# Serving the second layer's experts with 64 tokens each and no branches, the rest through the loop

## The chip, the cores and the metric

The kernel runs on one core of one Trainium2 chip. The metric is the device time of one execution in microseconds; three runs of the kernel before gave 1768.14, 1769.0 and 1769.58 us, median 1769.0.

## What is computed

Two layers of a transformer over 512 tokens and 256 context tokens of width 1024 in float32. Each layer has a mixer (attention beside a convolution or a pooling), then a mixture of experts. The part that matters here is the experts:

```python
def _moe(h, grp_w, grp_b, exp_w, exp_b, w_gate, w_up, w_down):
    ...
    hid = jax.nn.silu(xb @ w_gate[e]) * (xb @ w_up[e])
    return (hid @ w_down[e]) * wt[:, None]
```

There are 32 experts in 4 groups; a token takes one group and two experts of it, whose results are weighted and added. In the last layer only the 512 tokens take part: 1024 assignments, 32 an expert on average. Every expert's weights are read whole: gate and up 1024x512 each, down 512x1024, 6 MB in float32, 32 times in each layer.

## The kernel before

The weights of an expert are loaded as 12 tiles of 128x1024 float32, 512 KB each: chunks 0 and 1 (4 tiles each) hold gate and up, chunk 2 (4 tiles) holds down. They go to places of 4 KB a partition (`Pages`); a place that is given back by `used` is taken by the next load in the order of use (`ahead`, L1326 on), issued by SP (L1333) or, at the start, in part by ACT. The pool of the experts adds `NS[l]` places to those that are lasting; in layer 1 there are 3.

All engines but SP keep, in this stage, the order in which the program is written (`by_hand`); nothing reorders the instructions of an engine. `main` (the loop over `n` in `range(NE)`) takes the experts one after another, two experts (a pair, index `m`) sharing one gather:

- `gather0(m)` (POOL, L1352): the rows of up to 64 tokens of each of the pair's experts, one below the other in `Xg`. `gather1` does so for tokens 65 to 128, under a branch.
- `trans(m, b)` (`transposed`, L1460): 8 transpositions on PE into PSUM `xtp`, and 8 evictions by ACT (L689) and DVE (L687) in turn, with the norm's gain and shift, into `xt`. Block `b = 1` is transposed whether it holds tokens or not.
- `mm_gate_up(0, ...)` (L1476): per weight tile two products of 64 columns (32 records of a 128x512 float32 product an expert, as each product has two passes), then a branch on the expert's count for the second block.
- `hidden` (ACT L1481, DVE L1482) and `hidden_T` (4 transpositions L1489, copy L1494): the activation of both blocks, turned for the next product.
- `down(n - 1)` (L1500): the previous expert's down products, one expert behind. In layer 1 then `result` (DVE L1386: weight and gate), `parts` (ACT L1408, POOL L1409: the result as a high and a low part that PE multiplies exactly in one pass each), and a branch for a second block (`second`).
- `combine(m)` (L1426): at each even expert, the results of the pair before are added to their tokens: a one-hot matrix (`onehot`, DVE L1413) times high and low part, 8 units of two products, each added to `X` by DVE (L1390).

The last three experts (`TAIL`) have their second blocks deferred to one branch behind the last one. Experts with more than 128 tokens get the rest in the loop of `rest` (L1656 on), entered if the count of such blocks is not zero. `slots` computes each place's weight for both blocks with 16 products `wps` (L1271) before expert 0. A branch on several engines (L1294, L1296) splits the program; what is behind waits for what stands in front on that engine.

Of the kernel before, what the change touches and what calls it, by code (L numbers as in the profile page):

```python
# [7 lines left out]
F32 = mybir.dt.float32  # L8
# [60 lines left out]
def hybrid_dit_kernel(ctx: ExitStack, tc: tile.TileContext, a, out):  # L69
# [56 lines left out]
    def load(src, n=4, pools=None, queue=nc.sync):  # L126
        """The first n pages of a chunk of weights"""
# [75 lines left out]
    def gemv_first(n, w):  # L203
        """The shift and the scale of a pair of row blocks in layer 0's first norm"""
# [19 lines left out]
    def scale_cols(l, which):  # L224
        """ln gain * (1 + scale), one column a block of 128"""
# [8 lines left out]
    def mod_rows(l, name, src):  # L234
        """A vector of columns as rows in DRAM, to be read into all partitions."""
# [9 lines left out]
    def router_bias(l):  # L245
        """The router's logits of the second norm's shift, and its bias"""
# [12 lines left out]
    def rpow(work, ss, n, scale):  # L259
        """1/sqrt(ss * scale + eps)"""  # L260
# [14 lines left out]
    # A float32 is the sum of two parts of 12 bits each, which TensorE multiplies exactly in one pass each;  # L275
    # a product of two float32 takes three passes then: high * high, high * low and low * high.
    class Split:
        """A chunk of weights in its two parts, made page by page by the steps"""
# [20 lines left out]
        def __call__(self, p, k, o, n):  # L299
            """Columns o to o + n of row block k, part p"""  # L300
# [9 lines left out]
    rope = {}  # L310

    def rope_tables(l, pool, t0=0, n=XT):
        """Of tiles t0 to t0 + n"""
# [42 lines left out]
    def qk_rotate(l, t, n0, qn, W, mid):  # L356
        """Rotation and split of the normed queries and keys"""
# [1811 lines left out]
```

## Time and profile before

| what | value |
|---|---|
| runs | 1768.14, 1769.0, 1769.58 us |
| profiled execution, span | 1769.0 us (its own time is the same within the spread of the runs; the span is the median) |
| PE busy | 1567.2 us, 89% |
| PE weight loads (beside the products) | 866.9 us, 49% |
| DVE, ACT, POOL busy | 913.2, 528.4, 427.4 us |
| HBM read | 510.49 MB, 300 GB/s over the span |
| gate/up products, both layers (L1476) | 516.7 us busy, 2304 records |
| down products, both layers (L1500) | 264.8 us busy, 1152 records |

The page cuts the span into 40 slices of 44.2 us. The experts of layer 0 take about 440 to 960 us, those of layer 1 about 1245 to 1769. A busy share is an average over stages; the stage must be looked at by itself, with windows. Waits are listed as "who waited <- whom"; PEq and SPq are the sequencers of PE and SP, which branch and issue DMAs. Idle time shorter than about 0.15 us is not listed as a wait.

### The profile page before, as it was taken

The page shows a single profiled execution, that of the slowest core. Times are in us where ns is not written, and L with a number is a line of the kernel's source. Part 1 is how long each engine was busy: PE and PEld are TensorE (multiplying, and loading weights), DVE is VectorE, ACT ScalarE, POOL GpSimd, SP SyncE. Part 2 cuts the span into 40 slices and gives each one's busy share as a digit, 9 for nine tenths or more (in the row PEclk, how much of TensorE's full clock was granted, in tenths as well). Part 3 has the DMA queues.
Part 4 walks back from the last instruction along what each step waited for, and adds up shares of the span by engine and source line. Part 5 has one row for each costly group of instructions (what it writes and reads, how often), then busy time and mean ns, then how long its engine had stood idle before and what let it go on. Part 6 is the DMA issues. An engine that isn't in the chain of part 4 may idle for free. (4 is left out here: it accounts for less than half of the span.)

```text
span 1769.0 us, 24713 instructions
## 1 busy us (share of the span) xinstructions
PE 1567.2 (89%) x8732; PEld 866.9 (49%) x8732; DVE 913.2 (52%) x1747; ACT 528.4 (30%) x1036; POOL 427.4 (24%) x347
## 2 busy tenths in 40 slices
PE   5979689997899999998986789989799999989997
PEld 4867457885333333332321676677334344343442
DVE  3897889788333232322333656656534445344454
ACT  3422468733111111111112434663312122121221
POOL 1535556132112112211111223201121121111110
PEclk9999799999999999999999899999799999999999
DMA  9121743447999999999998338145699999999992
GB/s 368 58 83 66 292 155 122 164 148 278 354 396 397 388 390 386 391 394 389 392 400 332 123 108 319 58 180 188 257 408 408 408 408 406 408 406 406 405 407 91
DMA packets 151597, 519.03 MB, mean 293 GB/s; under 512 B 22445, under 2 KB 23181, under 8 KB 151437
## 3 DMA queue, kind: packets, MB, share of 16 engines
q1 hardware_dynamic: 134300, 479.67, 69.2%
q0 software_dynamic: 11520, 16.81, 3.7%
q10 hardware_dynamic: 5616, 20.45, 3.0%
q8 instruction: 97, 1.59, 0.4%
q14 instruction: 64, 0.52, 0.1%
HBM read 510.49 MB, written 21.02 MB: 300 GB/s over the span
## 5 line engine op out<-in xcount | busy, mean ns | idle before, releaser
L1476 PE MATMUL gu<-w,xt 128*64 128x512 f32 x2304 | 516.7, 597 | 21.1 <-DMA w<-in_ex_dram 11.9
L1476 PEld LDWEIGHTS gu<-w,xt 128*64 128x64 f32 x2304 | 171.5, 137 | 326.6 <-issue 247.6
L1500 PE MATMUL yy<-w,ht 128*64 128x512 f32 x1152 | 264.8, 601 | 14.2 <-PEq L1296 5.9
L1482 DVE TENSOR_TENSOR hh<-hh,gu 128x512 f32<-128x512 f32 x64 | 44.1, 688 | 451.6 <-ACT hh L1481 451.6
L1481 ACT ACTIVATE hh<-gu 128x512 f32<-128x512 f32 x64 | 38.3, 598 | 566.2 <-PEq L1296 416.2
L1500 PEld LDWEIGHTS yy<-w,ht 128*64 128x64 f32 x1152 | 81.4, 137 | 172.4 <-issue 133.7
L1379 POOL DMA_INDIRECT xD<-ys,sidx x40 | 70.6, 1765 | 317.8 <-DVE ys L1375 315.3
L1409 POOL TENSOR_TENSOR lo<-ys,hi 64x1024 fp32r<-64x1024 f32 x29 | 68.2, 2351 | 325.0 <-ACTq L1296 325.0
L749 DVE SCALAR_TENSOR_TENSOR acc<-glu,convp,acc 128x784 f32<-128x784 f32 x76 | 97.9, 1288 | 1.6
L760 POOL TENSOR_TENSOR part<-part,prod 128x784 f32<-128x784 f32 x40 | 84.7, 2118 | 43.2 <-ACT prod L759 42.2
L1375 DVE TENSOR_TENSOR ys<-yy,ys 128x512 f32<-128x512 f32 x64 | 44.3, 692 | 97.8 <-PEq L1296 53.4
L1408 ACT ACTIVATE hi<-ys 64x1024 fp32r<-64x1024 f32 (+1 forms) x35 | 34.4, 983 | 193.1 <-DVE ys L1386 108.8
L1352 POOL DMA_INDIRECT Xg<-hD,gidx x40 | 42.6, 1066 | 188.9 <-PE xtp L1460 179.7
L264 POOL TENSOR_TENSOR rs<-ms,mhalf 128x1 f32<-128x1 f32 (+2 forms) x40 | 41.5, 1038 | 170.8 <-DVE ms L262 170.3
L1390 DVE TENSOR_TENSOR X<-X,cmb 128x512 f32<-128x512 f32 x126 | 77.0, 683 | 1.6 <-PE cmb L1426 1.1
L1426 PE MATMUL cmb<-hi,oh 128*128 128x512 f32 x128 | 58.0, 453 | 22.2 <-DVE oh L1413 20.5
L1460 PEld LDWEIGHTS xtp<-cst,Xg 128*128 128x128 f32 x512 | 58.0, 146 | 34.6 <-PEq L1296 18.6
L1460 PE MATMUL xtp<-cst,Xg 128*128 128x128 f32 x512 | 64.8, 282 | 9.1 <-PEq L1296 9.1
L522 PE MATMUL ptp<-cst,P 128*128 128x128 f32 x368 | 53.3, 284 | 18.7 <-POOL P L510 10.5
L1494 DVE COPY ht<-htp 128x512 f32<-128x512 f32 x64 | 43.8, 684 | 50.0 <-PE htp L1489 50.0
L695 PE MATMUL qps<-wh,hi 128*128 128x256 f32 (+1 forms) x176 | 61.4, 349 | 8.0 <-DVE hi L1819 2.4
L687 DVE TENSOR_SCALAR xt<-xtp,A,modT 128x128 f32<-128x128 f32 x128 | 49.6, 410 | 35.7 <-ACT xt L689 34.6
(310 smaller groups left out, 2633.9 us busy)
## 6 DMA issues: line engine op xcount, KB each, us to landing
w<-in_ex_dram SPq DMA_DIRECT2D x751, 512.0 KB
w<-in_mod_w_dram SPq DMA_DIRECT2D x96, 512.0 KB
w<-in_ex_dram ACTq DMA_DIRECT2D x17, 512.0 KB
w<-in_w_out_dram SPq DMA_DIRECT2D x16, 512.0 KB
w<-in_w_in_ab_dram SPq DMA_DIRECT2D x14, 512.0 KB
hD<-x ACTq DMA_DIRECT2D x8, 512.0 KB
xD<-X ACTq DMA_DIRECT2D x6, 512.0 KB
w<-in_w_in_cd_dram ACTq DMA_DIRECT2D x6, 512.0 KB
```

The lines of the kernel that those rows point to most:

```text
L522: nc.tensor.transpose(ps[:, (c - c0) * 128:(c - c0 + 1) * 128], u["P"][c // nk][:, c % nk * 128:(c % nk + 1) * 128], ident)
L687: nc.vector.tensor_scalar(dst[:, k, :], src, g, b, op0=OP.mult, op1=OP.add)
L695: nc.tensor.matmul(ps[:, o:o + n], h(x, k, tk), w(p, k, 0, n), start=(k == 0 and c == 0), stop=(k == KT - 1 and c == 2))
L749: nc.vector.scalar_tensor_tensor(acc, glu[:, ct, i:i + CW], w(i), acc, OP.mult, OP.add)
L760: nc.gpsimd.tensor_tensor(self.part[ct], self.part[ct], t, OP.add)
L1379: return nc.gpsimd.indirect_dma_start(out=xD[:, :], out_offset=bass.IndirectOffsetOnAxis(ap=idx, axis=0), in_=ys[:, :], in_offset=None, bo ...
L1390: nc.vector.tensor_tensor(x, x, ps, OP.add)
L1409: eng.tensor_tensor(lo[rows, c], ys[rows, c], hi[rows, c].bitcast(F32), OP.subtract)
L1426: nc.tensor.matmul(ps, oh[:, tok(t)], y[:, c * 512:(c + 1) * 512], start=(i == 0), stop=(i == 1))
L1460: nc.tensor.transpose(ps[:, k * 128:(k + 1) * 128], src[:, (h * 4 + k) * 128:(h * 4 + k + 1) * 128], ident)
L1476: nc.tensor.matmul(self.gu[c * 64:(c + 1) * 64, b, :], xt[:, k, q * 64:(q + 1) * 64], w[k][:, c * 512:(c + 1) * 512], start=(k == 0), stop ...
L1500: nc.tensor.matmul(yy[c * 64:(c + 1) * 64], t[:, b, f % 2, f // 2, :], w[f][:, c * 512:(c + 1) * 512], start=(f == 0), stop=(f == 3))
```

## The change

In layer 1 an expert's own share is one block of 64 tokens (`FIRSTB = (2, 1)`); what is beyond 64 goes to `rest`, which so far served what is beyond 128. With that, layer 1 gets a loop of its own (`main1`) with no branches in it: no second gather, no second transposition, no second gate/up, hidden or down, and one branch behind the last expert. `hidden` and `hidden_T` work on half the columns. Gate/up and down alternate between two halves of their PSUM tiles. The one-hot is made before the down products of the same turn, and the 8 units of `combine` run inside the next expert's gate/up products: two units after each of its tiles 5, 6 and 7, the others behind. The products `wps`, 8 instead of 16, run behind expert 0's gate/up. The pool has 5 places instead of 3. Layer 0 keeps its loop (`main0`) and its order.

```diff
-NS = (9, 3)
+NS = (9, 5)
+FIRSTB = (2, 1)
...
-            pg = sm("pg")[:, :4 * NE]
-            for b in range(2):
+            pg = sm("pg")[:, :2 * self.nb * NE]
+            for b in range(self.nb):
...
-            for c in (slice(0, 512), slice(512, D)) if n >= TAIL else (slice(0, D),):
+            for c in (slice(0, 512), slice(512, D)):
...
-        def mm_gate_up(self, b, xt, q, w):
+        def mm_gate_up(self, b, xt, q, w, beside=lambda k: None):
             for k in range(KT):
                 for c in range(2):
                     nc.tensor.matmul(self.gu[c * 64:(c + 1) * 64, b, :], xt[:, k, q * 64:(q + 1) * 64],
                                      w[k][:, c * 512:(c + 1) * 512], start=(k == 0), stop=(k == KT - 1))
+                beside(k)
-        def hidden(self, nb):
-            hh = self.wp.tile([128, 2, 256], F32, tag="hh", name="hh", bufs=1)
-            nc.scalar.activation(hh[:, :nb], self.gu[:, :nb, 0:256], AF.Silu)
+        def hidden(self, b, nb):
+            hh = self.wp.tile([128, FIRSTB[self.l], 256], F32, tag="hh", name="hh", bufs=1 + self.l)
+            nc.scalar.activation(hh[:, :nb], self.gu[:, b:b + nb, 0:256], AF.Silu)
...
+        def begin(self):
...
+            products = self.route.slots(self.pool, self.wp, room)
+            if l == 0:
+                products()
+            self.trans(0, 0)
+            self.gather0(2)
+            if l == 0:
+                self.ahead(queue=nc.scalar)
+                self.trans(0, 1)
+            self.over = self.overflow(self.pool, self.route.cnt)
+            return products
...
+        def main1(self):
+            units = []
+            def beside(k):
+                for _ in range(2 if k >= 5 else 0):
+                    if units:
+                        units.pop(0)()
+            def down(n, then=lambda: None):
+                yy = self.yy[:, n % 2, :]
+                self.mm_down(yy, 0, hT[n], W[n, 2])
+                self.used((n, 2))
+                then()
+                self.parts(n, self.result(n, yy))
...
+            products = self.begin()
+            for n in range(NE):
+                m = n // 2
+                if n == NE - 1:
+                    down(n - 1)
+                self.mm_gate_up(n % 2, xT[m, 0], n % 2, W[n, 0] + W[n, 1], beside)
+                while units:
+                    units.pop(0)()
+                self.used((n, 0), (n, 1))
+                if n == 0:
+                    products()
+                    self.ahead()
+                hh = self.hidden(n % 2, 1)
+                if n % 2 and m + 1 < NP:
+                    self.trans(m + 1, 0)
+                    if m + 3 < NP:
+                        self.gather0(m + 3)
+                def turn():
+                    hT[n] = self.hidden_T(n, hh, 1)
+                if 0 < n < NE - 1:
+                    oh = self.pair_onehot(m - 1) if n % 2 == 0 else None
+                    down(n - 1, turn)
+                    if n % 2 == 0:
+                        units.extend(self.combine(m - 1, oh))
+                else:
+                    turn()
+            when(self.tail[0:1], COMPUTE + SP_ONLY,
+                 lambda: self.rest(self.wp, self.over, self.route.O, self.route.rank, self.nt))
+            oh = self.pair_onehot(NP - 1)
+            down(NE - 1)
+            for u in self.combine(NP - 1, oh, store):
+                u()
...
-            nlev = (self.ntok - 2 * BLK) // BLK
+            first = FIRSTB[self.l]
+            nlev = (self.ntok - first * BLK) // BLK
```

Two places show how instructions move. The first is PE's queue from an odd expert's gate/up to the next even one's down products. The names: `gu` gate/up, `xtp` transposed gathered rows, `yy` down, `htp` transposed hidden rows, `cmb` combining products, of which there are 16 in a row. Before:

```order
L1476 MATMUL gu<-w,xt_11794 64x512 x16
L1294 TENSOR_LOAD cnti
L1296 COMPARE_AND_BRANCH
L1476 MATMUL gu<-w,xt_11813 64x512 x16
L1296 UNCONDITIONAL_BRANCH x2
L1460 MATMUL xtp<-cst,Xg_11516 128x128 x8
L1460 MATMUL xtp<-cst,Xg_11518 128x128 x8
L1500 MATMUL yy<-w,ht 64x512
L1296 UNCONDITIONAL_BRANCH
L1500 MATMUL yy<-w,ht 64x512 x7
L1489 MATMUL htp<-cst,hh 128x128 x4
L1426 MATMUL cmb<-hi,oh 128x512
```

After, the same stretch:

```order
L1487 MATMUL gu<-w,xt_11693 64x512 x12
L1435 MATMUL cmb<-hi,oh 128x512
L1435 MATMUL cmb<-lo,oh 128x512
...
L1487 MATMUL gu<-w,xt_11693 64x512 x2
...
L1471 MATMUL xtp<-cst,Xg_11506 128x128 x8
L1509 MATMUL yy<-w,ht 64x512 x8
L1501 MATMUL htp<-cst,hh 128x128 x2
```

The products of the second block (skipped by the branch where the count is at most 64) and the branches are gone, the second eight transpositions too, and the combining products stand after 12, 14 and 16 gate/up products (six, seven and eight tiles) instead of behind the down products.

The second place is SP's queue where layer 1's weights are loaded. 14 loads stand ahead of these rows, and ACT issues four loads between them and expert 0's products before, two now. Before:

```order
L256 DMA g1b<-rowg_88 128x1024
L1333 DMA w<-in_ex_dram 128x1024 x3
L256 DMA g2b<-rowg_91 128x1024
L1333 DMA w<-in_ex_dram 128x1024 x10
L1296 UNCONDITIONAL_BRANCH x3
L1333 DMA w<-in_ex_dram 128x1024 x7
L1296 UNCONDITIONAL_BRANCH
```

After:

```order
L258 DMA g1b<-rowg_88 128x1024
L1342 DMA w<-in_ex_dram 128x1024 x3
L258 DMA g2b<-rowg_91 128x1024
L1342 DMA w<-in_ex_dram 128x1024 x365
L1303 TENSOR_LOAD tail
```

SP meets no branch between the loads any more. Of the 365, the first ten are those of before; the next three go to places that are free already (one of these was loaded by ACT before, two are new); the one after these is load 33 of 384 and waits for the first place that expert 0's products give back.

## Rows read from the trace of the kernel before

**Rows 1.** the page's 40 slices of 44.2 us: PE busy in tenths, and GB/s

```profile
PE   5979689997899999998986789989799999989997
...
GB/s 368 58 83 66 292 155 122 164 148 278 354 396 397 388 390 386 391 394 389 392 400 332 123 108 319 58 180 188 257 408 408 408 408 406 408 406 406 405 407 91
```

**Rows 2.** windows: length, busy us of each engine (x instructions), PE clock, DMA share, GB/s

```profile
1250.00:1260.00 10.00, 9.62 (x46) 5.58 (x48) 6.19 (x24) 3.44 (x8) 1.09 (x2) 0.69 0.45 153
1260.00:1270.00 10.00, 8.43 (x44) 2.82 (x40) 1.96 (x6) 0.60 (x1) 0.00 (x0) 1.00 0.62 234
1270.00:1724.00 454.00, 418.05 (x1962) 185.18 (x1960) 200.88 (x362) 98.09 (x178) 80.59 (x42) 1.00 1.03 407
...
1732.00:1734.00 2.00, 1.22 (x10) 0.48 (x8) 0.81 (x2) 0.00 (x0) 0.00 (x0) 1.00 0.06 25
```

**Rows 3.** waits of SP, 1270 to 1724 us: total, times, longest

```profile
SPq L1333 <- DMA w<-in_ex_dram: 309.7, 334, 2.0
SPq L1333 <- PEq L1296: 11.7, 15, 5.0
```

**Rows 4.** waits of PE, 1265 to 1721 us

```profile
PE cmb L1426 <- DVE oh L1413: 20.5, 14, 1.5
PE xtp L1460 <- PEq L1296: 4.4, 15, 0.3
PE gu L1476 <- PEq L1296: 3.7, 13, 0.5
PE yy L1500 <- PEq L1296: 3.6, 12, 0.3
PE gu L1476 <- DMA w<-in_ex_dram: 1.5, 5, 0.3
```

**Rows 5.** instructions of two lines, layer 1: duration ns min/median/max, first and last start

```profile
L1476 PE MATMUL gu<-w,xt x1024: 589/592/1116, 1254.8 to 1748.6; 128*64 128x512 f32 x171
...
L1352 POOL DMA_INDIRECT Xg<-hD,gidx x16: 992/1012/1647, 1244.5 to 1647.8; - x16
...
DMA to landing us min/median/max: 5.6/7.3/7.8
```

**Rows 6.** timeline at the first expert: start, us, engine, instruction [idle before <- releaser]

```profile
1244.45 1.18 POOL L1352 DMA_INDIRECT Xg<-hD,gidx  x1 [2.10 <-DVE wgd L1232]
...
1248.18 0.34 PE L1271 MATMUL wps<-slots 128*128 128x96 bf16 x2 [5.51 <-DVE slots L1269]
...
1251.26 3.64 PE L1460 MATMUL xtp<-cst,Xg 128*128 128x128 f32 x16
1254.83 7.75 PE L1476 MATMUL gu<-w,xt 128*64 128x512 f32 x32
...
1252.38 0.46 ACT L689 ACTIVATE xt<-xtp,modT,A 128x128 f32<-128x128 f32 x1 [6.09 <-PE xtp L1460]
...
1262.72 4.16 SPq L1333 DMA_DIRECT2D w<-in_ex_dram  x8
```

**Rows 7.** PE's groups, 1270 to 1724 us: count, busy us, mean ns, idle before

```profile
L1460 PE MATMUL xtp<-cst,Xg 128*128 128x128 f32 x240 | 29.1, 274 | 4.4 <-PEq L1296 4.4
```

**Rows 8.** timeline of the last loads and of expert 31

```profile
1720.52 4.17 SPq L1333 DMA_DIRECT2D w<-in_ex_dram  x4
...
1742.10 7.09 PE L1476 MATMUL gu<-w,xt 128*64 128x512 f32 x32
1750.70 0.66 PE L1489 MATMUL htp<-cst,hh 128*128 128x128 f32 x4 [1.51 <-DVE hh L1482]
1752.45 3.65 PE L1500 MATMUL yy<-w,ht 128*64 128x512 f32 x16 [1.10 <-DVEq L1296]
```

**Rows 9.** layer 0's last experts: two windows, and a row of PE's timeline

```profile
930.00:940.00 10.00, 7.66 (x32) 1.48 (x31) 1.36 (x2) 2.43 (x4) 0.00 (x0) 1.00 1.03 384
940.00:950.00 10.00, 7.52 (x28) 2.20 (x28) 3.30 (x5) 0.72 (x1) 1.81 (x1) 0.83 1.03 398
...
918.44 1.08 PE L1476 MATMUL gu<-w,xt 128*64 128x512 f32 x4 [1.41 <-DMA w<-in_ex_dram]
```

More of the change, by code (lines that the diff above doesn't have):

```diff
@@ L1417, in pair_onehot, with unit @@
             c = (m % 2) * 8 + m // 2
-            return self.onehot(self.route.tokp[:, 0, c:c + 1])
+            return self.onehot(self.route.tokp[:, c:c + 1])
         def combine(self, m, oh, then=None):
-            for c in range(2):
-                for t in range(self.nt):
-                    ps = sm("cmb")
-                    for i, y in enumerate(self.hl[m]):
-                        nc.tensor.matmul(ps, oh[:, tok(t)], y[:, c * 512:(c + 1) * 512], start=(i == 0), stop=(i == 1))
-                    if then and t % 3 == 1:
-                        x, y = X(t)[:, c * 512:(c + 1) * 512], self.wp.tile([128, D], F32, tag="ys", name="ys", bufs=1)[:, 0:512]
-                        nc.scalar.activation(y, ps, AF.Copy)
-                        nc.gpsimd.tensor_tensor(x, x, y, OP.add)
-                    else:
-                        self.add(t, c, ps)
-                    if then:
-                        then(t, c)
+            def unit(c, t):
+                ps = sm("cmb")
+                for i, y in enumerate(self.hl[m]):
+                    nc.tensor.matmul(ps, oh[:, tok(t)], y[:, c * 512:(c + 1) * 512], start=(i == 0), stop=(i == 1))
+                if then and t % 3 == 1:
+                    x, y = X(t)[:, c * 512:(c + 1) * 512], self.wp.tile([128, D], F32, tag="ys", name="ys", bufs=1)[:, 0:512]
+                    nc.scalar.activation(y, ps, AF.Copy)
+                    nc.gpsimd.tensor_tensor(x, x, y, OP.add)
+                else:
+                    self.add(t, c, ps)
+                if then:
+                    then(t, c)
+            return [lambda c=c, t=t: unit(c, t) for c in range(2) for t in range(self.nt)]
         def block(self, b, w, tk):
@@ L1489, in hidden_T @@
                     nc.tensor.transpose(ps[:, (2 * b + c) * 128:(2 * b + c + 1) * 128], hh[:, b, c * 128:(c + 1) * 128], ident)
[L1490 to L1493 removed]
+            t = self.wp.tile([128, FIRSTB[self.l], 2, 2, 64], F32, tag="ht", name="ht", bufs=1 + self.l)
             nc.vector.tensor_copy(t[:, :nb].rearrange("p b c g n -> p (b c g n)"), ps[:, :nb * 256])
@@ L1565, in main, with pair_col, gather0, gather1 @@
             self.ahead(FIRST[l][2], queue=nc.scalar)
-            self.route.slots(self.pool, self.wp, room)
-            pages.done([room])
-            trans(0, 0)
-            gather0(2)
-            self.ahead(queue=nc.scalar)
-            trans(0, 1)
-            over = self.overflow(self.pool, self.route.cnt)
-            gather1(1)
+            products = self.route.slots(self.pool, self.wp, room)
[3 more added lines that the diff above has]
+            self.gather0(2)
+            if l == 0:
+                self.ahead(queue=nc.scalar)
+                self.trans(0, 1)
+            self.over = self.overflow(self.pool, self.route.cnt)
+            return products
+        def pair_col(self, t, m):
+            c = (m % 2) * 8 + m // 2
+            return t[:, c:c + 1]
+        def gather0(self, m):
+            self.gather(self.Xg[0][m % 2], self.pair_col(gidx[:, 0], m))
+        def gather1(self, m):
+            c = (m % 2) * 8 + m // 2
+            when(cntp[0:1, c:c + 1], [POOL], lambda: self.gather(self.Xg[1][0], self.pair_col(gidx[:, 1], m)))
+        def trans(self, m, b):
+            self.xT[m, b] = self.transposed(self.Xg[b][m % 2 if b == 0 else 0], b)
+        def main(self):
+            (self.main0, self.main1)[self.l]()
+        def main0(self):
+            W, xT, hT = self.W, {}, {}
+            self.xT = xT
+            NP = NE // 2
+            def down(n):
+                t, e = hT[n], order[n]
+                self.mm_down(self.yy[:, 0, :], 0, t, W[n, 2])
+                when(cnti[0:1, e:e + 1], [PE], lambda: self.mm_down(self.yy[:, 1, :], 1, t, W[n, 2]))
+                self.used((n, 2))
+                self.scatter(n, 0)()
+                when(cnti[0:1, e:e + 1], [POOL], self.scatter(n, 1))
+            self.begin()
+            self.gather1(1)
             for n in range(NE):
@@ L1578, in main @@
                     down(n - 1)
-                    if self.l == 0:
-                        rest()
+                    self.rest(self.wp, self.over, self.route.O, self.route.rank, self.nt)
                 self.mm_gate_up(0, xT[m, 0], n % 2, w)
@@ L1643, in overflow @@
                 nc.vector.tensor_scalar(tot, tot, float(2 * BLK), None, op0=OP.mult)
-                for n in range(TAIL, NE):
-                    nc.vector.tensor_tensor(tot, tot, cnt[:, order[n]:order[n] + 1], OP.max)
                 nc.vector.tensor_copy(self.tail, tot)
```

174 lines of the change are left out of this document (65 added, 109 removed).

## The prediction

> **What bounds the kernel now.** I read the profile page's 40 slices first, since the change touches only the experts of layer 1 (the second layer), the last 12 slices or so. There [rows 1] PE is busy for 8 to 9 tenths of nearly every slice, and the DMA engines move 405 to 408 GB/s until the last one. So two resources are nearly full at once, and the first question is which of them the other waits for. The windows [rows 2] answer half of it: from 1270 to 1724 us the DMA share is 1.03 at 407 GB/s without a dip, while before that, from 1250 to 1270, it is 0.45 and 0.62. SP's waits [rows 3] say what paces the issues: 309.7 us, 334 times, for an earlier load to land, and 11.7 us for PE's branches. SP hardly ever waits for a place that PE has not yet given back. The weights come as fast as the DMA engines move them, and the lever on the DMA side is when the steady stream begins.
>
> PE, on the other hand, does not wait for those weights. Its waits in the steady stage [rows 4] are the one-hot (20.5 us) and its own branches (4.4 + 3.7 + 3.6 us); those for gate/up weights come to 1.5 us. At the end the distance shows: the last weight load is issued at 1724.7, the DMA traffic has died away by 1734 [rows 2], and PE multiplies with that tile only from 1752.45 on [rows 8]. PE runs some 20 us behind the weights for the whole stage, at a pace of its own that happens to equal that of the stream. So the present end is PE's: down products of expert 31 until 1756.1, then 12.9 us to the end at 1769.0. That span is also the median of the three runs, so the sum below needs no offset.
>
> **Is there any work for the loop?** The change serves 64 tokens an expert and gives the rest to a loop. The trace says there is no rest here: gate and up have 1024 matmul records in layer 1, 32 for each of 32 experts, and 16 gathers, one a pair [rows 5]; a second block would add 32 records and a gather. So the new loop is entered no more than the old branches were.
>
> **Term 1, PE's own pace.** Per pair of experts the change takes away: 8 of 16 transpositions of gathered rows, of which the row has 240 in 29.1 us, so 0.97 us [rows 7]; two of four transpositions of the hidden rows in each expert, at about 0.12 us apiece (the pace of the other transpositions), 0.48 us; the wait for the one-hot, 20.5/14 = 1.46 us, since the one-hot is now made ahead of the down products; three branch gaps of 0.3 us, of which a normal hand-over keeps perhaps half. Over the 456 us of [rows 4] that is 32.2 us of waits, 14.5 us and 7.4 us of transpositions: 54 us. It adds switches: the 16 combining products now stand in four groups between gate/up products, about six changes of kind a pair. Before, such a change costs nothing to 0.3 us; at 0.15 us it is 0.9 us a pair, 14 us in all. PE thus sheds about 40 us (bounds 54 and, were each switch 0.3 us and the drain of PSUM by DVE exposed too, 20). The combining products are hidden by nothing and cost PE what they cost before; DVE's additions for them lie beside PE's products.
>
> **Term 2, when the stream begins.** In the kernel before, the eight places of expert 0 are given back only behind the branch for its second block, so SP issues the next load at 1262.72 although the first products began at 1254.83 [rows 6]. The changed kernel has no branch there: each load waits for its own place's last product. What else moves at this point: the 16 transpositions become 8, so gate/up need not wait for the second half (1251.26 to 1254.83 on PE); the 16 products for the weights of the slots, which kept PE until 1251.2, go behind expert 0; three free places (two new ones, and one that ACT loaded late) are loaded by SP right behind its earlier loads, in the idle DMA time before 1245. The first gather starts at 1244.45 and gathers land in 5.6 to 7.8 us [rows 5, 6], so the transpositions begin between 1250 and 1252; I take 1250.7, later than the earliest since the extra loads share the engines. The first evictions end 1.6 us after the transpositions begin (1252.84 against 1251.26), the granted clock is not yet full (0.69 over 1250 to 1260 [rows 2]), and the first two pairs of products take some 1.7 us. The first place is free at about 1254.2 and the load issued at **1254.7**, 8.0 us earlier (bounds 1253 and 1257.6). From there each product group frees a place every 0.9 us and a load takes 1.3 us, so the stream doesn't run dry. It is thin once: expert 1's products must follow the moved products (from 1248.18 to the transpositions at 1251.26 before, so 3.1 us [rows 6]) by about 1266, when the eight loads are through; I count nothing and 2 us as the bound.
>
> **Term 3, the stream's length.** Before, loads 32 to 384 (31 are issued earlier, as the rows of the order count) run from 1262.7 to 1734: 471.3 us for 353, or 1.335 us each with the gathers between them. After the change load 33 is the first of the stream: 352 loads, 470.0 us. The last tile lands at 1254.7 + 470.0 = **1724.7**. Nothing in the change makes a load faster; SP's branches were waits beside a full queue.
>
> The row that this rests on is 407 GB/s. The Trainium skill, "DMA: Bandwidth & Descriptors", section "Bandwidth", gives two figures for one core, a fabric ceiling of 435 GB/s and an HBM share of about 358 GB/s. The trace lies between them and refutes the lower as a limit; the upper is taken up among the rivals.
>
> **Term 4, the tail.** If PE has caught up by then, the last expert follows the landings. Its eighth gate/up tile lands four loads, 5.3 us, before the last. With the combining products of pair 14 between the products (two groups for each of the last three tiles, and two more behind), gate/up and these are through about when the last tile lands; from the end of gate/up to the down products the trace has 3.3 us (1749.2 to 1752.45, with 1.5 and 1.1 us of waits [rows 8]), of which the narrower activations save about 0.5 and the activation overlaps the last combining products; I put the down products at 1.4 to 5.1 us after the last landing. The 12.9 us behind them stay: same scaling, same split, eight combining groups, stores. The end lies 18.0 us after the last landing (bounds 13.8, if only the last tile's products are left, and 22).
>
> **Sum.** PE alone would be done with the down products at 1756.1 - 2.5 (earlier start) + 3 (moved products) - 40 = about 1717; the stream makes it 1724.7 + 5.1 = 1730. The later decides: 1724.7 + 18.0 = 1742.7, so **1743 us**, 26 less. What PE sheds beyond 27 us is given back as waits for weights.
>
> **Edits costed at nothing.** Halved one-hots and places in the router shorten the chain to the first gather by a few tenths of a us, which lies within the bounds of the first load. Zeroing one buffer and two PSUM tiles less frees ACT at a time when its next work waits for DVE's routing. The split of the results into two parts, now in halves, lies beside PE; the combining products that need it come behind six of the next expert's eight gate/up tiles, 5.3 us of products, and were that cover gone they would wait for POOL. Layer 0 keeps its order.
>
> **Rivals.**
> *PE stays the bound.* Switches and PSUM cost more than the nearest rows show, and PE sheds 20 us instead of 40: down products end at about 1737, the kernel at 1750; with 15 us shed, 1755. For: PE is at 9.2 tenths now. Against: the 32 us of waits are plainly gone. 0.13.
> *The stream starts no earlier.* Something that the semaphores hide (the loads' slots, a late gather) keeps the first load near 1262: end at 1734 + 18 = 1752. For: the 31 loads ahead share their eight semaphores with the loads behind, which the trace of before does not test here. Against: every load waits for its own place's products alone, beside those semaphores, whose loads have landed by then (share 0.45 at 1250). 0.08.
> *A quicker stream.* The stream's mean of 407 GB/s holds the gathers and whatever SP loses at the branches (11.7 us of its waits [rows 3]); one per cent or two more is 5 to 9 us: 1734 to 1738. At 7% more the stream would take 440 us, PE's own work would set the end, and the time would be 1717 + 12.9 = 1730. By the page's higher figure above it is this far end. Against: 454 us without a dip at 407 [rows 2]. 0.04 outside my main case.
> *Slower than before: the clock.* Once PE waits for each tile, the granted clock could fall to the lower of its two levels, and products of 0.9 us a tile become 1.8, more than the 1.3 us of a load. PE's spare time before it reaches 1756 + 3.5 is 43 us, so it decides from 86 us of the stage at half clock on, 18%; with a quarter of the stage the end is near 1789. Layer 0's experts bear on this: there PE waits up to 1.41 us for weights, and the clock is 1.00 in one of the last windows and 0.83 in the other [rows 9], so 1.2 instead of 2.4 GHz for a third of 10 us. That is a few per cent of the stage, not 18. The Trainium skill, "TensorE: Matmul & The Clock Gate", section "HAM oscillation — how this bites in real kernels", says that products shorter than the DMA wait before them keep falling back to the lower clock. By that rule a wait like the one of 1.41 us, before 1.08 us of products, would do it if it came at every tile; the trace has it now and then, and keeps the full clock. 0.03.
> *The change doesn't do what it says*: an expert with more than 64 tokens would enter the loop, at 12 loads of 1.3 us a block with nothing beside them, 16 us and more each. The counts of [rows 5] exclude it for these inputs. 0.01.
>
> **How the numbers follow.** Forecast 0.71, the rivals as given. The forecast's own range is 1734 to 1749. Its lower end goes with a first load at 1253, a stream 1% quicker and a tail of 15; its upper with a first load at 1257.6, 2 us lost at expert 1 and a tail of 20. The range is widened to 1732 to 1757 for the quicker stream and for the first two rivals; the last two, and a far end of the first where PE sheds nothing, are left out. About 0.2%, or 3.5 us, is what a measurement of this kernel can tell from no change: faster 0.94, same 0.02 (that far end), slower 0.04 (the clock and the loop).
>
> **What would show it.** Right: the first weight load behind expert 0 issued near 1255, DMA share 1.03 from about 1257, the last landing near 1725; PE waits for weights of 5 to 20 us in the later half, PE below 9 tenths, waits for the one-hot gone; 18 us from the last landing to the end. Wrong: no waits for weights on PE (first rival), DMA idle until 1263 (second), a clock below 1.00 in the stage (fourth), records of the loop. A prediction error of more than 10 us would mean that I mis-sized the tail or that the stream's pace itself depends on what the change removes.

## The result, and the profile after

The changed kernel takes **1741.2 us** (1738.0 to 1745.9, 4 runs) against 1768.8 us: a ratio of 0.9844, 95% interval 0.9823 to 0.9864. Forecast were 1743 and a range of 1732 to 1757. The span of the profiled execution is 1742.5 us (its own time was 1744.4), so the parts below are compared with the span of 1769.0 us before.

The page's slices (43.6 us each now), PE busy and GB/s, answer to [rows 1]:

```profile
PE   5979689999699999999987689989699999999996
...
GB/s 370 63 72 62 314 134 147 106 181 220 357 393 399 399 384 385 394 388 390 399 393 397 219 73 175 243 71 137 309 409 408 409 409 409 409 409 408 409 408 249
```

The windows answer to [rows 2] (length, busy us of PE, PEld, DVE, ACT, POOL with instructions, PE clock, DMA share, GB/s):

```profile
1250.00:1260.00 10.00, 7.30 (x30) 3.40 (x32) 3.42 (x13) 1.72 (x4) 1.31 (x2) 0.67 0.48 150
1260.00:1270.00 10.00, 8.26 (x36) 2.81 (x34) 2.57 (x11) 0.38 (x1) 0.00 (x0) 0.84 0.99 388
1270.00:1450.00 180.00, 180.00 (x824) 69.10 (x822) 72.51 (x134) 33.37 (x67) 39.64 (x33) 1.00 1.03 408
1450.00:1700.00 250.00, 236.15 (x999) 78.34 (x994) 92.19 (x170) 40.39 (x81) 46.04 (x38) 1.00 1.03 408
1700.00:1710.00 10.00, 7.40 (x27) 1.87 (x27) 3.42 (x6) 1.25 (x2) 0.00 (x0) 0.86 1.03 407
...
1720.00:1722.00 2.00, 2.00 (x9) 0.95 (x9) 1.15 (x3) 0.38 (x1) 0.00 (x0) 1.00 0.45 184
1722.00:1724.00 2.00, 1.23 (x6) 0.67 (x4) 2.00 (x4) 0.00 (x0) 0.00 (x0) 1.00 0.05 16
```

The stream has the rate that it had, 408 GB/s for 407, but it stands at a share of 0.99 from 1260 on, where it was 0.62, and has died away by 1724, ten us earlier. PE, on the other hand, is busy without a gap until 1450 and then has 14 us to spare in 250. Its waits (total, times, longest; 1265 to 1715 us) answer to [rows 4] and say why:

```profile
PE gu L1487 <- DMA w<-in_ex_dram: 8.3, 38, 0.8
PE yy L1509 <- DMA w<-in_ex_dram: 4.6, 23, 0.2
PE yy L1509 <- DVE ys L1396: 2.1, 1, 2.1
PE htp L1501 <- DVE hh L1494: 1.1, 1, 1.1
```

The one-hot and the branches are gone as releasers; weights have taken their place. So the bound has passed from PE to the stream in the middle of the stage. How, the transpositions of the gathered rows show best: PE does them once a pair, behind the second expert's gate/up, so from one to the next is PE's time for a pair. Before (PE's timeline: start, us):

```profile
1424.32 1.94 PE L1460 MATMUL xtp<-cst,Xg 128*128 128x128 f32 x16 [0.30 <-PEq L1296]
...
1455.94 1.94 PE L1460 MATMUL xtp<-cst,Xg 128*128 128x128 f32 x16 [0.30 <-PEq L1296]
```

After:

```profile
1411.17 1.03 PE L1471 MATMUL xtp<-cst,Xg 128*128 128x128 f32 x8
...
1438.43 1.04 PE L1471 MATMUL xtp<-cst,Xg 128*128 128x128 f32 x8
...
1465.95 1.03 PE L1471 MATMUL xtp<-cst,Xg 128*128 128x128 f32 x8
```

A pair took PE 31.6 us and takes 27.3. I call **lag** the time from the landing of the pair's last gate/up load to this point, with landings counted in packets of the trace. Before, the lag stood at 21 us from the third pair to the last: the landings of a pair's 24 loads, 31.7 us apart, and PE kept equal paces. After, the landings are 31.5 us apart (13 pairs from 1269.5 to 1679.2), and the lag begins at 32.6 (the weights now run further ahead), shrinks by some 4 us a pair to 6.5 at 1466, and stays at 6.5 to 7.7, with pairs of 30.6 to 32.2 us: from there PE takes each tile as it lands.

The start of the stream, answering to [rows 6]:

```profile
1246.01 1.18 POOL L1362 DMA_INDIRECT Xg<-hD,gidx  x1 [2.72 <-DMA w<-in_ex_dram]
...
1252.70 1.97 PE L1471 MATMUL xtp<-cst,Xg 128*128 128x128 f32 x8 [9.17 <-DMA Xg<-hD,gidx]
1254.60 8.06 PE L1487 MATMUL gu<-w,xt 128*64 128x512 f32 x32
...
1256.61 1.27 SPq L1342 DMA_DIRECT2D w<-in_ex_dram  x2
```

The first load behind expert 0 follows the first products by 2.0 us, where it was 7.9. And the end, answering to [rows 8] (PE's rows, then DVE's):

```profile
1720.11 1.08 PE L1487 MATMUL gu<-w,xt 128*64 128x512 f32 x4
1724.74 0.44 PE L1501 MATMUL htp<-cst,hh 128*128 128x128 f32 x2 [1.52 <-DVE hh L1494]
1725.95 3.65 PE L1509 MATMUL yy<-w,ht 128*64 128x512 f32 x16 [0.77 <-DVEq L1305]
...
1721.88 2.48 DVE L1400 TENSOR_TENSOR X<-X,cmb 128x512 f32<-128x512 f32 x4 [0.85 <-PE cmb L1435]
1724.27 0.42 DVE L1494 TENSOR_TENSOR hh<-hh,gu 128x256 f32<-128x256 f32 x1
```

The last packet of a weight load ends at 1722.7 (before 1733.9), and the kernel ends 19.8 us later (before 35.1). The 26.5 us are thus: 6.1 from the first load (1262.7 to 1256.6), 5.1 from the stream's length (471.2 to 466.1), 15.3 from what follows the last landing. These are parts of a sum and not causes that could each be had alone; the experiments say which of them needs which.

### The profile page after: what moved, and what is told of

Read it like the earlier page. It is cut to its first block, busy times and chain, and to the rows that moved or that the text cites. A ratio compares the mean times of both kernels' runs of the same rounds, so it can differ in the third digit from the quotient of the medians.

```text
span 1742.5 us, 23633 instructions
## 1 busy us (share of the span) xinstructions
PE 1562.7 (90%) x8524; PEld 827.3 (47%) x8524; DVE 869.7 (50%) x1674; ACT 497.9 (29%) x998; POOL 430.1 (25%) x376
## 5 line engine op out<-in xcount | busy, mean ns | idle before, releaser
L1487 PE MATMUL gu<-w,xt 128*64 128x512 f32 x2304 | 536.7, 604 | 23.1 <-DMA w<-in_ex_dram 18.9
L1494 DVE TENSOR_TENSOR hh<-hh,gu 128x512 f32<-128x512 f32 (+1 forms) x64 | 35.4, 553 | 358.4 <-ACT hh L1493 358.4
L1493 ACT ACTIVATE hh<-gu 128x512 f32<-128x512 f32 (+1 forms) x64 | 31.4, 490 | 606.9 <-PE gu L1487 345.4
L1419 POOL TENSOR_TENSOR lo<-ys,hi 64x512 fp32r<-64x512 f32 x58 | 72.6, 1269 | 216.5 <-ACT hi L1418 216.5
L1418 ACT ACTIVATE hi<-ys 64x512 fp32r<-64x512 f32 x64 | 40.2, 629 | 138.4 <-DVE ys L1396 138.4
L1503 DVE COPY ht<-htp 128x512 f32<-128x512 f32 (+1 forms) x64 | 35.4, 553 | 66.7 <-PE htp L1501 65.5
L532 ACT ACTIVATE pT<-ptp 128x512 f32<-128x512 f32 (+1 forms) x96 | 53.5, 589 | 48.7 <-PE ptp L524 47.8
L512 POOL TENSOR_SCALAR P<-P,rd 128x768 f32<-128x768 f32 (+3 forms) x40 | 34.1, 853 | 134.4 <-DVE rd L510 40.3
L502 ACT ACTIVATE P<-S,nm 128x768 f32<-128x768 f32 (+3 forms) x80 | 59.9, 757 | 12.9 <-DVE nm L495 8.0
L495 DVE TENSOR_REDUCE nm<-S 128x1 f32<-128x768 f32 (+3 forms) x80 | 58.7, 764 | 9.4 <-PE S L488 5.9
```

The costliest lines, as they stand in the source:

```text
L495: nc.vector.tensor_reduce(nm, u["S"][h][:, u["span"]], AX.X, OP.max, negate=True)
L502: nc.scalar.activation(u["P"][h][:, :n], u["S"][h][:, u["span"]], AF.Exp, bias=nm, accum_out=u["den"][:, h:h + 1])
L532: nc.scalar.activation(dst, src, AF.Copy)
L1419: eng.tensor_tensor(lo[rows, c], ys[rows, c], hi[rows, c].bitcast(F32), OP.subtract)
L1487: nc.tensor.matmul(self.gu[c * 64:(c + 1) * 64, b, :], xt[:, k, q * 64:(q + 1) * 64], w[k][:, c * 512:(c + 1) * 512], start=(k == 0), stop ...
```

## The experiments

Theory: the stream sets the end; its earlier start and the shrunken lag of PE are the gain. Rivals: PE's shed work by itself; the two extra places; the new order of the combining products. Each kernel is the changed one with one edit. The table has what the profiled executions and the times say, in us; "first load" counts from the first gate/up product, "stream" from there to the last weight packet, "tail" from that to the end; "sum" is the three together, "last lag" the lag at the last pair. The first gate/up product itself comes between 1247 and 1255 us, since the program ahead of it varies by execution; this shifts everything behind it, and the sum is free of it: e11 and e12, whose medians lie 4.5 us apart, differ by 0.2 us in the sum. But each kernel has one profiled execution, so no run shows how far the sum itself scatters.

| kernel | first load | stream | tail | sum | pair on PE | last lag | time | ratio to before |
|---|---|---|---|---|---|---|---|---|
| before | 7.9 | 471.2 | 35.1 | 514.2 | 31.6 | 21.1 | 1768.8 | |
| changed | 2.0 | 466.1 | 19.8 | 487.9 | 27.3 | 7.1 | 1741.2 | 0.9844 (0.9823 to 0.9864) |
| e1, 3 places | 2.0 | 470.1 | 21.3 | 493.4 | 27.3 | 7.5 | 1744.7 | 0.9863 (0.9841 to 0.9885) |
| e2, 6 places | 2.0 | 465.9 | 21.3 | 489.3 | 27.3 | 7.6 | 1741.8 | 0.9840 (0.9821 to 0.9859) |
| e3, first branch | 9.6 | 466.4 | 19.8 | 495.8 | 27.3 | 7.6 | 1749.0 | 0.9896 (0.9874 to 0.9917) |
| e4, combine apart | 2.0 | 468.3 | 45.5 | 515.9 | 31.4, 32.6 | 37.2 | 1769.6 | 1.0001 (0.9990 to 1.0012) |
| e5, combine in a block | 2.0 | 466.5 | 24.0 | 492.5 | 26.9 | 7.6 | 1745.0 | 0.9863 (0.9847 to 0.9879) |
| e6, transpose twice | 2.0 | 467.0 | 20.6 | 489.6 | 28.2 | 7.8 | 1742.1 | 0.9854 (0.9839 to 0.9868) |
| e7, transpose thrice | 2.0 | 466.9 | 46.5 | 515.4 | 31.1, 32.8 | 32.1 | 1771.4 | 1.0022 (1.0007 to 1.0038) |
| e8, branch each, taken | 9.2 | 475.7 | 34.6 | 519.5 | 28.2, 34.5 | 24.4 | 1775.0 | 1.0042 (1.0029 to 1.0055) |
| e9, branch each, not taken | 7.9 | 468.5 | 21.2 | 497.6 | 28.2 | 9.0 | 1747.4 | 0.9873 (0.9851 to 0.9895) |
| e10, last combine later | 2.0 | 466.1 | 19.4 | 487.5 | 27.3 | 7.6 | 1738.4 | 0.9837 (0.9816 to 0.9859) |
| e11, that and 6 places | 2.0 | 464.8 | 18.6 | 485.4 | 27.3 | 7.7 | 1736.4 | 0.9825 (0.9800 to 0.9850) |
| e12, last combine spread | 2.0 | 465.2 | 18.3 | 485.6 | 27.3 | 7.6 | 1740.9 | 0.9833 (0.9814 to 0.9851) |

**e1 and e2, the places.**

```diff
-NS = (9, 5)
+NS = (9, 3)
```

and `(9, 6)`.

> The second layer's experts get 3 places of their own again instead of 5. Theory (from expert 15 on the stream of loads sets the end): two more of the loads fall behind the first expert, 354 for 352, so 2 x 1.335 = 2.7 us later than the changed kernel, 1744 for 1741. Rival (TensorE's own work sets the end): 1741, no change. Rival (the two extra places bring most of the gain, since TensorE runs dry without them): 1750 or more.

> One place more, 6 for 5. Theory (the stream sets the end): one load less behind the first expert, 1.3 us sooner, 1740. Rival (TensorE's work sets the end): 1741.

e1 came out 3.4 us above the changed kernel: the stream is 4.0 us longer, of which its two further loads explain 2.7. That fits the theory and excludes the rival of 1750; from no change the two intervals don't separate it. For e2 the times say nothing (+0.6); its stream is 0.2 us shorter. The tails of both are 1.5 us longer, and that is not the places: the waits ahead of the last down products are those of the changed kernel, 1.5 and 0.8 us, but then the granted clock falls to the lower of its two levels, and the products take 5.35 us for 3.65. In e1 (PE's row, then two windows):

```profile
1724.46 5.35 PE L1509 MATMUL yy<-w,ht 128*64 128x512 f32 x16 [0.77 <-DVEq L1305]
...
1724.00:1726.00 2.00, 1.54 (x6) 0.60 (x7) 0.63 (x2) 0.00 (x0) 0.00 (x0) 0.69 0.04 8
1726.00:1728.00 2.00, 2.00 (x8) 0.83 (x6) 0.00 (x0) 0.00 (x0) 0.00 (x0) 0.50 0.00 0
```

From the start of these products to the end is 16.5 us in the changed kernel and wherever the clock stays up; it is 18.2 in e1 and e2 and 18.1 in e9. The two places that e1 lacks are thus worth 3 to 4 us, about two loads; what the one more of e2 is worth doesn't show.

**e3, the first branch back.**

```diff
                 self.mm_gate_up(n % 2, xT[m, 0], n % 2, W[n, 0] + W[n, 1], beside)
+                if n == 0:
+                    when(cnti[0:1, order[n]:order[n] + 1], [PE],
+                         lambda: self.mm_gate_up(1 - n % 2, xT[m, 0], n % 2, W[n, 0] + W[n, 1]))
```

> Behind the gate and up products of the first expert alone stands the branch of the kernel before again (TensorE reads the count and jumps over a second block's products), so the first expert's places come back only behind the branch. Theory (the stream sets the end, and its start is part of the gain): the first load behind expert 0 is issued near 1263 for 1256.6, the last load lands 5 to 7 us later, and the end with it: 1746 to 1749. Rival (the gain is TensorE's shed work alone): the branch itself, 1 to 2 us, at most hidden behind TensorE's lag, so 1741 to 1743.

The edit did more than it was meant to: `cnti` still holds the first layer's counts, the branch was taken, and PE did 32 further products, into a bank that nobody reads. PE's and SP's rows:

```profile
1247.16 15.54 PE L1487 MATMUL gu<-w,xt 128*64 128x512 f32 x64
...
1256.74 1.19 SPq L1342 DMA_DIRECT2D w<-in_ex_dram  x2
```

It tells the two theories apart all the same, and better than planned. In this execution the first products came 7.4 us earlier than in the changed kernel's; the first load left at the same moment (1256.7 for 1256.6) and the kernel ended at the same moment (1742.9 for 1742.5). Neither PE's earlier start nor its 7.5 us of added work shows in the end; the first load alone does. Over the runs it is 7.7 us slower, and the sum is 7.9 us longer.

**e8 and e9, a branch behind every expert but the last.** The edit of e3 with `n < NE - 1`; e9 also copies the second layer's counts into `cnti`, so that no branch is taken.

> The branch over a second block's gate and up products stands behind every expert but the last. Theory (its cost is the late return of the first expert's places, 7.7 us in the run with that branch alone; TensorE's waits at the others, 3.7 to 12 us in the rows of the kernel before, fit in what it has to spare): 1748 to 1752. Rival (31 branches hold TensorE beyond its room, or hold the places back at every expert): 1757 or more.

> As the run with a branch behind every expert but the last, but the branches read the second layer's own counts, so that none is taken (in the run before this they read the first layer's counts and eight were taken). Theory (what the branches cost is the late return of the first expert's places; TensorE's gaps of about 0.3 us each fit in the 4.3 us a pair that it has to spare beside the stream): the pair takes 27.9 to 28.5 us until TensorE catches up, the first load behind expert 0 comes about 6 us later, the end 5 to 8 us later, 1746 to 1750. Rival (branches that are not taken cost as much as those that were, or hold the places back all along): 1757 or more.

In e8 the first layer's counts sent eight experts into the body (1280 gate/up matmuls for 1024), and a pair with one takes 34.5 us for 28.2: the run says nothing of a branch that is not taken, and the rival's number in it proves nothing. e9 does:

```profile
1251.49 7.76 PE L1489 MATMUL gu<-w,xt 128*64 128x512 f32 x32
...
1259.39 2.92 SPq L1344 DMA_DIRECT2D w<-in_ex_dram  x6
```

The first load comes when the whole expert is through, 7.9 us after its first products, to the tenth what the kernel before had. A pair takes 28.2 us on PE, 0.9 more, and PE still catches up, at 1472. The median is 6.1 us higher, where the theory said 5 to 8, though the interval overlaps that of the changed kernel. The sum is 9.7 us longer: 5.9 at the first load, 2.4 in the stream, 1.4 in the tail, and the last is the clock again (the last down products take 5.21 us). So most of what the branches cost is the delay of the first load; their gaps on PE are absorbed. The 2.4 us in the stream seem to be theirs too: e3, with a first load as late and one branch, has 466.4. In e9 SP waits for PE's branches 10 times, 9.2 us in all and once 7.1 us, behind the second expert, where the DMA share falls to 0.91 (1275 to 1280 us); in e3 it has no such wait.

**e4 and e5, the combining products.**

```diff
-                        units.extend(self.combine(m - 1, oh))
+                        for u in self.combine(m - 1, oh):
+                            u()
```

for e4, and for e5

```diff
-                for _ in range(2 if k >= 5 else 0):
+                for _ in range(0):
```

> The combining products of a pair run in one piece right behind the down products, not between the next expert's gate and up products. Theory (the stream sets the end): what TensorE loses by it, up to 1.3 us a pair in the rows of the kernel before (20.5 us of waits for the one-hot matrix and the evictions over 16 pairs), disappears in the 20 us that TensorE now waits for weights: 1741 to 1745. Rival (putting them between is what pays): 15 pairs at 1.3 us, 1755 to 1761.

> The combining products of a pair run in one piece behind the next expert's gate and up products, when their two parts are long made. Theory A (the 28 us of the run with the products right behind the down products are its 41 us of TensorE waits for the parts just made, less about 13 us that TensorE has to spare beside the stream): without those waits only the pace of the evictions is left, at most the 20.5 us of such waits in the kernel before, 1741 to 1749. Theory B (alternating the products with gate and up products is itself what pays): 1757 to 1770.

e4 gives the whole gain back, so the theory as I had priced it missed, by 25 us. What I had left out: in that place the products need the two parts of the expert just done, which in the kernel before they did not. The waits of PE in e4, 1265 to 1735 us, and three windows of one pair:

```profile
PE cmb L1435 <- ACT hi L1418: 29.3, 15, 2.0
PE cmb L1435 <- POOL lo L1419: 11.7, 14, 0.8
```

```profile
1382.00:1384.00 2.00, 0.71 (x4) 0.20 (x2) 1.18 (x3) 0.01 (x1) 0.00 (x0) 1.00 1.03 412
1384.00:1386.00 2.00, 0.50 (x1) 0.19 (x1) 0.74 (x1) 1.24 (x2) 1.31 (x2) 0.82 1.02 408
1386.00:1388.00 2.00, 1.99 (x5) 1.61 (x6) 0.99 (x2) 0.00 (x0) 1.20 (x1) 0.50 1.03 410
```

Two waits of 1.95 and 0.84 us a pair, and then the granted clock at the lower of its levels for several us, in which combining products follow one another in 0.43 us instead of 0.23: the pair is 31.4 us long, or 32.6 where the clock stays low for longer, the lag stays at 36 to 37 us from the third pair on, and what the lag keeps is paid after the last landing (tail 45.5). The stream starts as early as in the changed kernel and is as long, within 2.2 us, and yet the sum is that of the kernel before. e5, with the same products in one piece but their parts long made, decides between theories A and B: its pair takes 26.9 us, *less* than the changed kernel's 27.3, and the time is 1745.0, as A said. So alternating them with gate/up products saves PE nothing in the steady stage; it is the later place that pays. The median is 3.8 us higher, with overlapping intervals; in the profile the difference arises at the end alone (tail 24.0 for 19.8), where all eight pairs of products, and DVE's eight additions, stand between the last gate/up and the hidden rows. Three of its windows, and its last down products:

```profile
1722.00:1724.00 2.00, 0.10 (x1) 0.00 (x0) 2.00 (x4) 0.00 (x0) 0.00 (x0) 1.00 0.00 0
1724.00:1726.00 2.00, 1.14 (x4) 0.53 (x6) 0.95 (x3) 0.00 (x0) 0.00 (x0) 0.63 0.03 8
1726.00:1728.00 2.00, 2.00 (x8) 0.65 (x6) 0.00 (x0) 0.00 (x0) 0.00 (x0) 0.50 0.00 0
...
1725.30 6.64 PE L1509 MATMUL yy<-w,ht 128*64 128x512 f32 x16 [0.77 <-DVEq L1305]
```

PE has nothing to do while DVE adds, the clock falls to 0.50, and the down products take 6.64 us for 3.65. They begin 0.6 us later behind the last landing than in the changed kernel; the other 3.6 us come behind their start, with the clock.

**e6 and e7, more work for PE.**

```diff
                     self.trans(m + 1, 0)
+                    for _ in range(1):
+                        self.transposed(self.Xg[0][(m + 1) % 2], 1)
```

and `range(2)`.

> Each pair's eight transpositions and evictions are done twice, the second time into a tile that nobody reads: 120 transpositions of 0.12 us more, about 15 us of TensorE. Theory (the stream sets the end, TensorE has about 13 us to spare): 1741 to 1745. Rival (TensorE's own work sets the end): 1756.

> The same transpositions three times, about 30 us more of TensorE than the changed kernel. Theory (13 us to spare, then TensorE sets the end one for one): 1756 to 1760. Rival (the stream sets the end with much more room): 1741 to 1746. Rival (TensorE's own work sets the end): 1771.

e6 is as expected: about 14 us more on PE, 0.8 us in the time, the lag near its floor at 1496 instead of 1466. e7 is not: I had taken each set for 15 us, but the third has to wait for the evictions of the second. Of PE's timeline in e7:

```profile
1393.26 2.00 PE L1471 MATMUL xtp<-cst,Xg 128*128 128x128 f32 x16
1396.20 0.66 PE L1471 MATMUL xtp<-cst,Xg 128*128 128x128 f32 x4 [0.94 <-DVE xt L689]
1397.48 0.66 PE L1471 MATMUL xtp<-cst,Xg 128*128 128x128 f32 x4 [0.63 <-DVE xt L689]
...
1424.37 2.01 PE L1471 MATMUL xtp<-cst,Xg 128*128 128x128 f32 x16
```

The pair takes 31.1 us and twice 32.8, where the granted clock falls for a while, on the mean 31.4 (from 1299.9 to 1707.8 in 13 pairs), the pace of the stream; the lag stays at 32 us to the end, and the time is 30 us longer. It meets the number of the rival that has PE set the end throughout, but e6 excludes that rival. My "13 us to spare" was also wrong: it was PE's waits for weights, whereas the room is what the lag and these waits absorb together. e6 has used 0.9 of the 4.3 us a pair, e7 and e4 all of it. Both of these have the early first load (2.0 us) and end as late as the kernel before: while PE needs the stream's time for a pair, an earlier stream only lengthens the lag. Where between them the cost begins, no run shows.

**e10, e11 and e12, the end.**

e10 holds back the last four combining products of pair 14, two into the wait for the hidden rows and two behind their transposition:

```diff
-                for _ in range(2 if k >= 5 else 0):
+                for _ in range(2 if k >= 5 and (k < 7 or len(units) > 4) else 0):
...
-                while units:
+                while units and n < NE - 1:
...
                 else:
+                    for u in units[:2]:
+                        u()
                     turn()
+                    for u in units[2:]:
+                        u()
```

e11 is that with `NS = (9, 6)`. e12, also with 6 places, puts one behind each of the last expert's tiles (`range((k > 0) if last[0] else 2 if k >= 5 else 0)`) and gives the down products of expert 30 a bank of their own (`sm("yy")`).

> At the last expert the four combining products that ran behind its gate and up products come later: two while VectorE multiplies the hidden rows, two behind the transposition. Theory (after the last landing the end waits for VectorE, which adds four products to the rows, 2.48 us, before it multiplies the hidden rows): the hidden rows are ready 2 to 2.6 us sooner, the down products begin 1 to 2 us sooner, the time from the last landing to the end falls from 19.8 to about 18: 1739. Rival (the down products follow the last landing, not VectorE): no change, 1741.

> The same with one place more for the second layer's experts, 6 for 5, so that one load less falls behind the first expert. Theory (stream and tail set the end, each by itself): 1.3 us less than the run before it, 1738. Rival (a place more gives nothing, as the run with it alone seemed to say): 1739 to 1740.

> As the run before it (6 places), but at the last expert the eight combining products come one behind each gate and up tile from the second on, in TensorE's waits for the landings, the eighth while the hidden rows are made; and the down products of expert 30 have a bank of their own in place of one that shares its tile with the bank that VectorE still reads (a wait of 2.08 us in the run before). Theory (at the end TensorE's and VectorE's leftover work lies behind the landings, and can be brought ahead of them): down products begin about 2.5 us sooner after the last landing, 1733 to 1734. Rival (what is brought forward only delays gate and up by as much): 1736.

The medians of e10 and e11 are 2.8 and 4.8 us below the changed kernel's, as forecast, but the intervals overlap with its own, so neither is shown to be faster than the change. The profile of e10 confirms the step in the main (DVE's row, PE's, and a window further on):

```profile
1716.03 0.42 DVE L1494 TENSOR_TENSOR hh<-hh,gu 128x256 f32<-128x256 f32 x1 [0.62 <-ACT hh L1493]
...
1719.28 3.65 PE L1509 MATMUL yy<-w,ht 128*64 128x512 f32 x16 [1.41 <-DVEq L1305]
...
1726.00:1728.00 2.00, 2.00 (x6) 1.59 (x5) 0.88 (x3) 0.60 (x1) 0.25 (x1) 0.50 0.13 50
```

DVE now multiplies the hidden rows right behind the activation, 1.0 us before the last landing instead of 1.6 behind it, and the down products begin 2.2 us behind the landing instead of 3.3. The rest is lost to a new wait: the down products stand behind the branch to the loop, and there PE waits 1.41 us, until DVE has made the two additions that were moved ahead of it. That the tail is 19.4 for 19.8 all the same is the clock, which falls during the combining products at the very end; e11, with the same end and the clock at 1.00 there, has 18.6, so the step is worth about 1 us. e12 gave nothing beyond e11: the median is back at 1740.9, and the sum is the same within 0.2. Tile and pair of combining products take 1.67 us of PE together there, against 1.33 us between two landings, so that what was brought forward delays gate/up by as much, as the rival said. The version with the lowest median of all is e11, at 1736.4 us (1735.4 to 1743.9).

## Why the prediction was right, step by step

- **The sum.** First load + stream + tail: forecast 1254.7 + 470.0 + 18.0 = 1742.7, measured 1256.6 + 466.1 + 19.8 = 1742.5. The bound is the one that was named, and the loop is not entered (1024 gate/up matmuls). That the total agrees to 0.2 us is luck: the terms are off by +1.9, -3.9 and +1.8. It is luck as well that the sum, which is a span, could stand for a time without an offset: the time of this execution is 1.9 us above its span, and the median of the runs lies 3.2 us below that time.
- **Term 2, the start.** The mechanism holds (2.0 us from the first products to the first load; e3 and e9 move the end by moving this load). The 1.9 us are the gather: it was issued at 1246.0 instead of 1244.45 [rows 6] and its transpositions began at 1252.7, not 1250.7. In the profiles of the other kernels with this start the first load leaves between 1251.0 and 1255.0 us, so how near 1254.7 comes is a matter of the execution. Expert 1 lost nothing in the stream, whose share is 0.99 from 1260 on.
- **Term 3, the length.** 352 loads at 1.324 us for 1.335. The text put the difference among the rivals, as "whatever SP loses at the branches". e9 has the gate/up branches again and a stream of 468.5, e3 one of them and 466.4, so some 2 of the 3.9 us are probably theirs; the rest I did not settle.
- **Term 1, PE's own pace, was mis-sized,** and outside its bounds: 4.3 us a pair over 15 pairs are 64 us shed, not 40 (20 to 54; the 54 count the branch gaps whole, though the text lets a hand-over keep half of them). e5 shows that the six switches a pair, entered at 0.9 us, cost 0.4, and e9 that two branches a pair cost 0.9 where I let a hand-over keep half of three gaps. With 0.45 us for each of the four branches that a pair had (two behind gate/up, two behind the down products) the sum is 1.45 + 1.46 + 1.8 - 0.4 = 4.3 us; that is an estimate, since no experiment put those behind the down products back. The error did not reach the time, since the stream was the later of the two anyway.
- **Term 4, the tail.** 19.8 for 18.0, within its bounds, but one step in it failed. The forecast had the down products from 1.4 to 5.1 us after the last landing; they run from 3.3 to 6.9, and that is the whole of the 1.8 us. It let the activation overlap the last combining products and left out DVE, which adds four of these, 2.48 us, before it multiplies the hidden rows; e10 moves the additions, and the down products come 1.1 us sooner. The clock is a second thing that the term left out: e1 and e2, with the same end, have a tail of 21.3 where it falls.
- **What would show it.** PE waits 12.9 us for weights, within the 5 to 20 us; the one-hot is gone. PE below 9 tenths was wrong: it is at 9.4 from 1450 to 1700, though it needs 27.3 of 31.5 us, since the products of a tile that come by themselves count as 1.08 us busy, and as 0.89 in a row (7.09 us for eight tiles [rows 8]).
- **The rivals.** *PE stays the bound* is what e4 and e7 became, at 4.1 to 4.5 us a pair more. *The stream starts no earlier* is what e9 tried: the span of its profiled execution is 1749.1, not 1752, with 3.3 us less at the first load than the rival's 1262.7, because the first products came as much sooner, and a stream 2.8 us shorter and a tail 3.2 us longer than its terms. *The clock* did not fall in the stage (1.00 in both windows), though PE waits for tiles, 0.8 us at most; it is 0.84 before it (1260 to 1270) and 0.86 behind it (1700 to 1710), around the wait of 2.1 us ahead of expert 30's down products. In the experiments it did cost time, in the stage in e4 and in the tails of others, up to 3.6 us in e5.

## What to carry to other kernels

Where an engine and a stream are both full, compare their times for one unit of work (here 31.6 and 31.7 us a pair before, 27.3 and 31.5 after) and follow the lag of the one behind the other: a lag that stays is paid after the last landing, a lag that shrinks shows who will bound the end. Work taken off the engine is then worth at most what the lag can shrink by, 14 us here (21.1 to 7.1) of 64 shed; the rest of the gain lies in when the stream begins and how long it is, and it can be had only once the engine is the quicker of the two (e4 and e7 have the early stream and gain nothing). And look what a branch reads before it is put back for an experiment: in two of these runs it was taken.

## What the runs showed of the hardware that I had not expected

- In e4 a wait of 1.95 us, a product, and a wait of 0.84 us stand once a pair between 28 us of dense products, and behind them the clock falls to its lower level each time (0.50 of full speed at 1386): the pair is 4.5 to 5.7 us longer than in e5, where the clock stays up until 1724, for 2.8 us of waits. The single wait of 1.46 us a pair for the one-hot [rows 4] left the clock of the kernel before at 1.00 [rows 2]. Nor do the waits alone decide it: behind the same 1.5 and 0.8 us ahead of the last down products it stayed at 1.00 in the changed kernel and fell in e1, e2 and e9. The Trainium skill, "TensorE: Matmul & The Clock Gate", section "HAM oscillation — how this bites in real kernels", tells of kernels whose products are shorter than the waits between them; here, in e4, they are ten times as long, and the clock falls all the same, for some us.
- The stream of one core stood at 408 GB/s for 450 us. The Trainium skill, "DMA: Bandwidth & Descriptors", section "Bandwidth", gives a core's HBM share as about 358 GB/s when both cores of a pair stream; this kernel runs on one core, and that figure was no limit in any of the runs.
